# Pacing the early adding transfers by DVE's results as well as by ACT's copies

## The chip, the cores and the metric

The kernel runs on one core of one Trainium2 chip. Its engines run side by side, each with an instruction queue of its own: TensorE (PE, with its weight loads shown as PEld), VectorE (DVE), ScalarE (ACT), GpSimd (POOL) and SyncE (SP). SP issues most of the DMA transfers, POOL issues those that add into memory and some stores. The metric is the time of one execution on the device, in microseconds, as the median of several runs. Before the change it is 960.55 us (three runs, 957.44 to 962.81).

## The reference, cut to what matters

One encoder layer over 1024 tokens of width 1024, all in float32:

```python
h = rmsnorm(x, norm_g)
q, k, v, za, u, vs, zs, gm = split(h @ w_in)
a = window_sink_attention(rope(q), rope(k), v, sinks)       # 16 heads, 2 key heads, window 128
a = (a * silu(za)) @ w_att_out
s = chunked_spatial_gating(gelu(u), gelu(vs), sg_w, sg_b, ln_g, ln_b)
s = (s * silu(zs)) @ w_sg_out
ga, gs = split(sigmoid(gm + b_merge))
out = rmsnorm(x + (ga * a + gs * s) @ w_o, final_g)
```

## The kernel before, in words

Each float32 operand of a product is split into a high and a low part, so that one product of two matrices is three matmuls per slice. Large products are made in pairs of 128-row strips of the weights by a scheme with seven products in place of eight (`gemm_pair`). A product is 12 matmuls of 128x512 (L320), so a pair is 84. Seven forms of the activations (b11, t1, t2, b21, t3, b22, t4) are kept for a whole stage. Of the weights each pair needs seven forms too: four quarters that come from memory and four sums of them, one quarter being used in the sums alone.

The sums are made in one of two ways. `pair_job` loads the quarters into the buffers `wr` (there are three) and adds them on DVE (`sums`, L233 to L236), one pair or more ahead of use. The buffers and the splitting are driven by `split_next`, which is called at fixed places of a pair and, when few split strips are left, starts the next job: its loads are issued on SP as soon as a buffer is free, and its sums stand on DVE near the end of the pair. `early_job` does without DVE: its sums are made far ahead in device memory, by six DMA transfers on POOL, of which the later ones add to what lies there. Ten jobs are made this way, and the sums of the output weights (`o_sums`) by 16 further transfers: 76 in all, in the list `early`. The first read of a sum comes near the end of the attention stage, at 608.9 us.

The list is worked off at hooks, places behind each of the seven products of a pair (and in the first stage behind groups of products). `part_of_early` takes the next transfer from the list and issues it on POOL. So that the transfers do not all start at once, each waits for an instruction that was remembered last in `pace[0]` (`paced`, by a dependency with a semaphore). In `gemm_pair` the remembered ones are ACT's three copies out of PSUM: L338 after product 0, L342 after product 1, L345 after product 2. The results of products 3, 4 and 5 are added on DVE (L350, L355, L359), and product 6 goes to the stage's own `finish`.

The stages in order, with the times of the profiled execution: normalising, keys, values and the first half of the gate's input up to about 136 us (the early list starts at 92.6 us, one transfer at every second group of products, paced by PE); the U stage to about 229 us (four pairs, spatial mixing beside them, one transfer at every hook, through `both`); the Q stage without early transfers; then the attention stage, from about 330 to 645 us. There the attention of 16 heads is cut into steps (`attention`, a generator) that are worked in at the hooks of eleven pairs, and `part_of_early` is called at each hook from the second of these pairs on and issues a transfer at every second one. What follows (att-gate pairs, the two output projections and the last product with the residual) issues none.

Two more places read `pace[0]`. `gate_of` (L1222 and on) orders the sigmoid of a gate on ACT behind the last remembered instruction by an edge that gives order without a semaphore (`after`). And the last stage sets and reads it for itself.

On POOL, behind the early transfers, stand the stores of the attention's results (L1075), which wait for DVE's additions (L1073). On DVE, in the attention stage, stand the products' additions, the softmax's maximum (L1011) and scaling, the splits' low parts (L154) and the weight sums. The order of the instructions on each engine is made by the framework's planner from the written order, the dependencies and its estimates of durations; it need not be the written order.

Of the kernel before, what the change touches and what calls it, by code (L numbers as in the profile page):

```python
# [54 lines left out]
def hybrid_tile(  # L55
# [16 lines left out]
    nc = tc.nc  # L72
# [12 lines left out]
    def bank(tag, dt=F32):  # L85
        return psum.tile([P, 512], dt, name=nm("ps_" + tag), tag="ps_" + tag, bufs=2)

    def mtile(shape, dt, tag, bufs, pool=None):
        return (pool or main).tile(shape, dt, name=nm(tag), tag=tag, bufs=bufs)
# [7 lines left out]
    def xtile():  # L97
        return mtile([P, HALF], F32, "x", 5)
# [57 lines left out]
    def after(second, first):  # L156

        tc.add_manual_dep(
            second.ins,
            first.ins.name,  # L160
            mybir.DependencyInfo(mybir.DependencyClass.NoSync, mybir.DependencyReason.DATA),
            reason="order",
        )
# [41 lines left out]
    def split_next():  # L205

        if not units:
            begin_job()
        if not units:
            return  # L210
        halves, keys = units.pop(0)
        hi = mtile([P, D], F32R, "wh", 3)
        lo = mtile([P, D], F32R, "wl", 3)
        if isinstance(halves, list):
            for c, half in enumerate(halves):
                split(hi[:, half_of(c)], lo[:, half_of(c)], half)
        else:
            wide = halves.shape[1]
            split(hi[:, 0:wide], lo[:, 0:wide], halves)
        for c, key in enumerate(keys):  # L220
            ready[key] = hi[:, half_of(c)], lo[:, half_of(c)]
        if len(units) == 1:
            begin_job()
# [33 lines left out]

    early = []
    pace = [None]

    def paced(move):

        if pace[0] is not None:
            tc.add_manual_dep(
                move.ins,
                pace[0].ins.name,
                mybir.DependencyInfo(mybir.DependencyClass.Sync, mybir.DependencyReason.DATA),
                reason="pace",
            )
# [42 lines left out]
    def product(acc, part, form, fresh, last=True):  # L312
        wh, wl = part
        bh, bl = form
        for k in range(4):
            ks = slice(k * P, (k + 1) * P)
            for n, (lt, rt) in enumerate(
                ((wh[:, ks], bh[:, k, :]), (wh[:, ks], bl[:, k, :]), (wl[:, ks], bh[:, k, :]))
            ):
                nc.tensor.matmul(  # L320
                    acc,
                    lt,
                    rt,
                    start=fresh and k == 0 and n == 0,
                    stop=k == 3 and n == 2,
                    skip_group_check=True,
                )

    def gemm_pair(b, finish, hook=lambda: None, second="o"):

        n = done[0]
        done[0] += 1
        acc = bank("mm")[:]
        x11, x12, x22 = xtile(), xtile(), xtile()
        product(acc, ready[n, 0], b["b11"], True)
        pace[0] = nc.scalar.copy(x11[:], acc)  # L338
        hook()
        t5 = bank("o")[:]  # L340
        product(t5, ready[n, 2], b["t1"], True)
        pace[0] = nc.scalar.mul(x22[:], t5, -1.0)  # L342
        hook()
        product(acc, ready[n, 3], b["t2"], False)
        pace[0] = nc.scalar.copy(x12[:], acc)  # L345
        split_next()
        hook()
        t2 = bank(second)[:]
        product(t2, ready[n, 1], b["b21"], True)
        nc.vector.tensor_add(x11[:], x11[:], t2)  # L350
        finish(0, 0, x11, x11[:], 1.0)
        split_next()
        hook()
        product(acc, ready[n, 4], b["t3"], False)
        nc.vector.tensor_sub(x22[:], x22[:], acc)  # L355
        finish(1, 1, x22, x22[:], 1.0)
        hook()
        product(t5, ready[n, 5], b["b22"], False)
        nc.vector.tensor_add(x12[:], x12[:], t5)  # L359
        finish(0, 1, x12, x12[:], 1.0)  # L360
        split_next()
        hook()
        product(acc, ready[n, 6], b["t4"], False)
        finish(1, 0, xtile(), acc, -1.0)
        split_next()
        hook()
# [381 lines left out]
    def hook():  # L748
        for _ in range(2):
            if late:  # L750
                late.pop(0)()
# [69 lines left out]
    for m in range(0, KC, 2):  # L821

        def finish(i, half, q, src, sign, m=m):
            nc.scalar.activation(q[:], src, AF.Gelu, scale=sign)
            late.append(lambda: mix(m + i, half, q))

        if m % 4 == 0:
            late.append(lambda m=m: bias.append(bias_of(m // 4)))
        gemm_pair(hb, finish, both)
# [87 lines left out]
    for m in range(0, KC, 2):  # L917

        def finish(i, half, q, src, sign):
            if sign < 0:  # L920
                nc.scalar.mul(q[:], src, sign)
            put(q_raw, m + i, half, q[:])
            rows = slice((m + i) * P, (m + i + 1) * P)
            split_q(q[:], [(slice(0, P), q_hl[:, rows, half_of(half)].rearrange("a p t -> p a t"))])

        if m == 2:
            steps_of_q.append(rope_tables())
        if m == 4:
            steps_of_q.append(rotate(0))
        gemm_pair(hb, finish, part_of_q)  # L930
# [39 lines left out]
    def zs_pair(m, hook, *place):  # L970
        quarters = []
        gemm_pair(hb, lambda *quarter: quarters.append(quarter), hook)
        for i, half, q, src, sign in quarters:
            nc.scalar.activation(q[:], src, AF.Silu, scale=sign)
        for i, half, q, src, sign in quarters:
            g = get(s1_dr, m + i, half, *place)
            nc.vector.tensor_mul(q[:], q[:], g[:])
            put(s_dr, m + i, half, q[:])
# [243 lines left out]
    def gate_of(src, m, i, half, col):  # L1222

        g = gates.pop(0)
        c = col + m + i
        gate = nc.scalar.activation(g[:], g[:], AF.Sigmoid, bias=bm_sb[:, c : c + 1])

        after(gate, pace[0])
        return g

    def gated(q, src, sign, g):
# [6 lines left out]
    for m in range(0, KC, 2):  # L1238
        if m == 2:
            a_q = {}  # L1240
            ahead_of_time += loads_of_quarters(a_q, a_dr)
        if m == 6:
            a_forms = forms_of(a_q)
            next(a_forms)

        def finish(i, half, q, src, sign):
            gated(q, src, sign, gate_of(gs_dr, m, i, half, KC))
            put(y_dr, m + i, half, q[:], nc.gpsimd)
            gates.append(get(gs_dr, m + 2 + i, half, 4) if m < 6 else get(ga_dr, i, half, 4))

        gemm_pair(sb_, finish, part_of_loads, "tp")
# [58 lines left out]
    for m in range(0, KC, 2):  # L1310
        if m == 6:
            written[0] += 1
            had = [raw_tile() for _ in range(2)]
            for i in range(2):
                copy_to(had[i][:], y_dr[(m + i) * P : (m + i + 1) * P, :])

        def finish(i, half, q, src, sign):
            gated(q, src, sign, gate_of(ga_dr, m, i, half, 0))
            if m < 6:
                add_to(place(y_dr, m + i, half), q[:])  # L1320
                gates.append(get(ga_dr, m + 2 + i, half, 4))
            else:
                nc.vector.tensor_add(q[:], q[:], had[i][:, half_of(half)])
                if half == 1:
                    last_rows[i] = q
                copy_to(place(y_dr, m + i, half), q[:])

        if m == 2:
            ahead_of_time += [lambda name=name: load_o(name) for name in list(O_SOURCES)[:4]]
        gemm_pair(ab, finish, part_of_loads, "tp")  # L1330
# [22 lines left out]
    for p in range(4):  # L1353
        acc = bank("sc" if p < 2 else "mm")[:]
        x11 = mtile([P, HALF], F32, "g", 4, pool)
# [7 lines left out]
    for p in range(4):  # L1363
        n, t, acc, x11 = N_PAIRS + p, T_ORDER[p], accs[p], firsts[p]
# [6 lines left out]
        x12, x22 = xtile(), xtile()  # L1371
# [32 lines left out]
        t5 = bank("o")[:]  # L1404
# [129 lines left out]
```

## Time and profile before

| what | value |
|---|---|
| median of the runs | 960.55 us (957.44 to 962.81, three runs) |
| the profiled execution's own time | 963.5 us |
| its span, first to last instruction | 961.7 us |
| PE, DVE, ACT, POOL busy | 97%, 72%, 58%, 13% of the span |
| granted TensorE clock, mean | 0.993 |
| moved by DMA | 198.64 MB, mean 207 GB/s |
| of it by POOL's queue (q0), by SP's (q1) | 48.24 MB, 149.28 MB |
| early transfers | 40 + 20 into `sums`, 12 + 4 into `g` |

The page of a profile lists busy times by engine, the span in 40 slices, the DMA queues, the chain of work that ended last, and the costliest groups of instructions. Other views answer questions on a stretch: the table by stage (busy time of each engine, granted clock, DMA share and GB/s), who waited for whom, and the instructions in order of time. A row of the latter reads: start us, duration us, engine, line, operation, output<-input, shapes, count, and in brackets how long the engine stood idle before it and what ended that. PE's matmuls overlap, so a PE that is busy without a break is not for that reason at its peak, but an idle PE is time lost. A name such as `wr` is a tile by the program's name without its buffer number; `g` stands both for the gates' tiles and for the output weights' sums in memory.

### The profile page before, as it was taken

Reading aid. Unit: us, or ns where it says so; the run is one execution under the profiler, and the core shown is the slowest. Engines: PE = TensorE matmul, PEld = TensorE weight load, DVE = VectorE, ACT = ScalarE, POOL = GpSimd, SP = SyncE. Lnnn points to the kernel's source line nnn. Section 1 sums busy time; section 2 is a strip of 40 time slices with the busy share of each in tenths; the row PEclk is TensorE's granted clock in tenths of the full one; section 3 lists DMA queues with packets and bytes.
Section 4 is the critical chain, followed back from the end, with each engine's and each line's share of the span. In section 5 each row is a group of like instructions: output and inputs, shape, how many; then the busy total and the mean of one; then the engine's idle time right before and its main releaser. Section 6 shows DMA issues by size and latency. Waiting matters only on the chain.

```text
span 961.7 us, 13452 instructions
## 1 busy us (share of the span) xinstructions
PE 931.4 (97%) x4465; PEld 769.7 (80%) x4465; DVE 691.0 (72%) x1322; ACT 557.9 (58%) x1061; POOL 122.6 (13%) x202
## 2 busy tenths in 40 slices
PE   8999999999999999999999998999999999999996
PEld 6888888888878778788878886888887887787885
DVE  6655576666675778788878876755589489568985
ACT  7864343333444479977767675754475565457443
POOL 2111222220000001111101021000110011210011
PEclk9999999999999999999999998999999999999999
DMA  7444767887769557876566695849758757979732
GB/s 277 124 137 137 209 216 177 181 166 181 247 204 315 188 183 205 224 194 162 157 215 216 206 219 134 217 145 326 281 199 311 281 195 252 264 191 297 232 113 87
DMA packets 126550, 198.64 MB, mean 207 GB/s; under 512 B 11409, under 2 KB 59281, under 8 KB 126481
## 3 DMA queue, kind: packets, MB, share of 16 engines
q1 hardware_dynamic: 108864, 149.28, 46.8%
q0 software_dynamic: 17472, 48.24, 21.2%
q8 instruction: 35, 0.57, 0.3%
q14 instruction: 35, 0.28, 0.1%
q10 hardware_dynamic: 144, 0.26, 0.1%
HBM read 141.65 MB, written 85.46 MB: 236 GB/s over the span
## 4 chain that ended last, share of the span: by engine, by line
PE 44%; DVE 9%; DMA 5%; ACT 4%; issue 3%; SPq 0%; POOL 0%; DVEq 0%; POOLq 0%; ACTq 0%
PE ps_mm L320 18%; PE ps_o L320 15%; DMA wr<-in_w_dram 3%; PE ps_sc L1009 3%; PE ps_o L1068 2%; PE ps_tp L1049 2%; DVE wl L154 2%; PE ps_tp L320 2%; PE ps_sc L320 2%; DMA wr<-y_dr 1%; DVE bq L183 1%; ACT pr L1021 1%; ACT wh L153 1%; DVE T_b22l L154 0%; DMA g<-s_dr 0%
## 5 line engine op out<-in xcount | busy, mean ns | idle before, releaser
L153 ACT CAST wh<-s 128x1024 fp32r<-128x1024 f32 (+1 forms) x76 | 75.9, 1001 | 93.6 <-PE ps_mm L320 44.1
L153 ACT CAST wh<-wr 128x1024 fp32r<-128x1024 f32 (+1 forms) x78 | 64.4, 828 | 74.0 <-PE ps_mm L320 32.9
L154 DVE TENSOR_TENSOR wl<-wr,wh 128x1024 fp32r<-128x1024 f32 (+1 forms) x78 | 73.8, 948 | 44.4 <-ACT wh L153 43.8
L154 DVE TENSOR_TENSOR wl<-s,wh 128x1024 fp32r<-128x1024 f32 (+1 forms) x76 | 88.4, 1164 | 15.1 <-ACT wh L153 13.6
L1021 ACT ACTIVATE pr<-pr,sm 128x256 f32<-128x256 f32 (+1 forms) x128 | 62.5, 490 | 24.2 <-DVE sm L1011 23.8
L1011 DVE CUSTOM_DVE_ANT_0 pr<-ps_sc,mask,nsink_sb 128x256 f32<-128x256 f32 (+1 forms) x128 | 56.2, 462 | 14.2 <-PE ps_sc L1009 13.6
L320 PE MATMUL ps_o<-T_t1h,wh 128*128 128x512 f32 x144 | 57.3, 398 | 0.9 <-ACT wh L153 0.9
L320 PE MATMUL ps_mm<-T_t4h,wh 128*128 128x512 f32 x136 | 54.3, 399 | 3.8 <-DVE x L355 3.8
L320 PE MATMUL ps_mm<-T_b11h,wl 128*128 128x512 f32 x136 | 54.3, 399 | 3.3 <-DVE wl L154 3.3
L320 PE MATMUL ps_o<-T_b22h,wh 128*128 128x512 f32 x144 | 57.4, 399 | 0.0
L320 PE MATMUL ps_o<-T_b22h,wl 128*128 128x512 f32 x144 | 56.9, 395 | 0.0
L1009 PE MATMUL ps_sc<-k,q 128*128 128x256 f32 (+1 forms) x256 | 48.6, 295 | 8.3 <-DVE sm L1011 8.2
L1009 PEld LDWEIGHTS ps_sc<-k,q 128*128 128x128 f32 x256 | 40.6, 190 | 19.9 <-DVE sm L1011 15.9
L320 PE MATMUL ps_o<-T_b22l,wh 128*128 128x512 f32 x144 | 56.5, 393 | 0.0
L320 PE MATMUL ps_o<-T_t1h,wl 128*128 128x512 f32 x144 | 56.4, 391 | 0.1
L320 PE MATMUL ps_o<-T_t1l,wh 128*128 128x512 f32 x144 | 56.1, 390 | 0.0
L320 PE MATMUL ps_mm<-T_b11h,wh 128*128 128x512 f32 x136 | 54.7, 402 | 0.7 <-ACT wh L153 0.7
L320 PE MATMUL ps_mm<-T_b11l,wh 128*128 128x512 f32 x136 | 53.9, 396 | 0.0
L320 PE MATMUL ps_mm<-T_t2h,wh 128*128 128x512 f32 x136 | 53.4, 393 | 0.1
L320 PE MATMUL ps_mm<-T_t3h,wh 128*128 128x512 f32 x136 | 53.5, 394 | 0.0
L320 PE MATMUL ps_mm<-T_t4h,wl 128*128 128x512 f32 x136 | 53.2, 391 | 0.0
L320 PE MATMUL ps_mm<-T_t4l,wh 128*128 128x512 f32 x136 | 53.2, 391 | 0.0
(369 smaller groups left out, 2517.3 us busy)
## 6 DMA issues: line engine op xcount, KB each, us to landing
wr<-in_w_dram SPq DMA_DIRECT2D x82, 256.0 KB
sums<-in_w_dram POOLq DMA_DIRECT2D x20, 512.0 KB, 5.6
s<-sums SPq DMA_DIRECT2D x20, 512.0 KB
s_dr<-x SPq DMA_DIRECT2D x32, 256.0 KB
q_hl<-qhl SPq DMA_DIRECT2D x16, 512.0 KB
q<-q_hl SPq DMA_DIRECT2D x64, 128.0 KB
wr<-in_w_dram SPq DMA_DIRECT2D x14, 512.0 KB
y_dr<-x POOLq DMA_DIRECT2D x28, 256.0 KB, 5.6
```

Source lines behind the costliest of these rows:

```text
L153: nc.scalar.copy(hi, src)
L154: nc.vector.tensor_sub(lo, src, hi.bitcast(F32))
L183: op(dst[:, i : i + 2, :], a[:, i : i + 2, :], c[:, i : i + 2, :])
L320: nc.tensor.matmul(acc, lt, rt, start=fresh and k == 0 and n == 0, stop=k == 3 and n == 2, skip_group_check=True,)
L1009: nc.tensor.matmul(sc[:, js], qt[:, i, :], kt[:, f, k0:], start=f == 0, stop=f == 1)
L1011: nc.vector.tensor_tensor_reduce(pr[:, i, k0:], sc[:, js], mask[:, k0:], 1.0, nsink_sb[:, h : h + 1], op0=ALU.add, op1=ALU.min, accum_out= ...
L1021: nc.scalar.activation(pr[:, i, k0:], pr[:, i, k0:], AF.Exp, bias=nmax[:, i : i + 1], scale=-1.0, accum_out=sums[:, i : i + 1],)
L1049: nc.tensor.transpose(pt[:, i * P : (i + 1) * P], pr[:, i, kt * P : (kt + 1) * P], ident[:])
L1068: nc.tensor.matmul(po[:], vv, parts[kt][:, n, :], start=kt == tiles[0] and n == 0, stop=kt == 1 and n == 1)
```

## The change

The additions of products 3, 4 and 5 on DVE are remembered in `pace[0]` too, so that a transfer issued at a hook waits for the result of the product just in front of it. The last hook of a pair, behind product 6, has no result of its own to remember and waits for the addition of product 5. The gate's order on ACT is kept at the last copy (L345), through a new variable `copied`. The transfers, their order and their places in the list stay as they are.

```diff
     pace = [None]
+    copied = [None]
...
         product(acc, ready[n, 3], b["t2"], False)
-        pace[0] = nc.scalar.copy(x12[:], acc)
+        pace[0] = copied[0] = nc.scalar.copy(x12[:], acc)
         split_next()
         hook()
         t2 = bank(second)[:]
         product(t2, ready[n, 1], b["b21"], True)
-        nc.vector.tensor_add(x11[:], x11[:], t2)
+        pace[0] = nc.vector.tensor_add(x11[:], x11[:], t2)
         finish(0, 0, x11, x11[:], 1.0)
         split_next()
         hook()
         product(acc, ready[n, 4], b["t3"], False)
-        nc.vector.tensor_sub(x22[:], x22[:], acc)
+        pace[0] = nc.vector.tensor_sub(x22[:], x22[:], acc)
         finish(1, 1, x22, x22[:], 1.0)
         hook()
         product(t5, ready[n, 5], b["b22"], False)
-        nc.vector.tensor_add(x12[:], x12[:], t5)
+        pace[0] = nc.vector.tensor_add(x12[:], x12[:], t5)
         finish(0, 1, x12, x12[:], 1.0)
...
-        after(gate, pace[0])
+        after(gate, copied[0])
```

## The prediction

> **What bounds the kernel now.** I read the page first (busy shares), then the stages that hold the change, then who waited for whom in them, then the queues around the one stall that this shows.
>
> ```profile
> span 961.7 us, 13452 instructions
> ...
> PE 931.4 (97%) x4465; PEld 769.7 (80%) x4465; DVE 691.0 (72%) x1322; ACT 557.9 (58%) x1061; POOL 122.6 (13%) x202
> ```
>
> TensorE (PE) is busy for 931.4 of 961.7 us, so no change of pacing can win more than the 30 us in which it idles, plus what a lowered clock costs. The table by stage shows how little of that lies where the adding transfers run. Columns: stretch, length, then busy us of PE, PEld, DVE, ACT and POOL, granted clock, DMA share, GB/s.
>
> ```profile
> 136.00:217.00 81.00, 81.00 (x405) 67.88 (x405) 55.36 (x85) 28.20 (x41) 22.45 (x28) 1.00 0.79 174
> ...
> 340.00:360.00 20.00, 18.63 (x88) 15.20 (x88) 14.11 (x46) 16.76 (x43) 0.00 (x0) 0.91 0.59 193
> 360.00:412.00 52.00, 50.45 (x257) 41.81 (x256) 43.78 (x111) 50.98 (x104) 8.27 (x10) 1.00 0.79 212
> ...
> 570.00:580.00 10.00, 6.82 (x36) 5.43 (x34) 4.57 (x8) 4.60 (x8) 0.82 (x1) 0.95 1.02 306
> 580.00:590.00 10.00, 9.24 (x36) 7.65 (x37) 7.16 (x20) 4.78 (x15) 0.00 (x0) 0.71 0.08 24
> ```
>
> The U stage (136 to 217) has PE busy for all of its 81 us. The attention stage (about 340 to 645) loses 1.55 us of PE in 360 to 412 and 3.18 + 0.76 = 3.94 us in 570 to 590, where the granted clock also falls to 0.95 and 0.71: 0.5 + 2.9 = 3.4 us of full clock. That one place costs up to 7.3 us. Its chain:
>
> ```profile
> 568.76 0.68 DVE L355 TENSOR_TENSOR x<-x,ps_mm 128x512 f32<-128x512 f32 x1
> ...
> 572.27 0.69 DVE L359 TENSOR_TENSOR x<-x,ps_o 128x512 f32<-128x512 f32 x1 [1.17 <-PE ps_o L320]
> ...
> 574.27 1.28 DVE L154 TENSOR_TENSOR pT<-ps_tp,pT 128x512 fp32r<-128x512 f32 x2
> 579.61 0.69 DVE L233 TENSOR_TENSOR s<-wr 128x512 f32<-128x512 f32 x1 [4.06 <-DMA wr<-in_w_dram]
> ```
> ```profile
> 580.76 0.50 PEld L1009 LDWEIGHTS ps_sc<-k,q 128*128 128x128 f32 x2 [4.37 <-DVE sm L1011]
> ```
>
> DVE is done at 574.27 + 1.28 = 575.55, stands 4.06 us before the first sum of the next pair's weights (L233, waiting for a weight load), and the attention scores behind it on PE wait for DVE's maximum (L1011) queued after that sum. The load was issued at 570.86 and took 8.67 us; at 406.00 an equal one took 4.17:
>
> ```profile
> 570.86 8.67 DMA wr<-in_w_dram
> ```
> ```profile
> 406.00 4.17 DMA wr<-in_w_dram
> ```
>
> Why so long? POOL's queue, how long its three transfers took, and the two DMA queues from 570 to 572 (packets, MB, share of the time of 16 engines):
>
> ```profile
> 562.16 2.52 POOL L412 DMA_DIRECT2D g<-in_w_dram  x3 [7.55 <-ACT x L345]
> 571.40 0.82 POOL L1075 DMA_DIRECT2D at_dr<-aT  x1 [6.72 <-DVE aT L1073]
> ```
> ```profile
> DMA to landing us min/median/max: 7.2/9.2/12.1
> ```
> ```profile
> q0 software_dynamic: 99, 0.34, 99.7%
> q1 hardware_dynamic: 36, 0.02, 5.0%
> ```
>
> ACT's copy at L345 released three 512 KB adding transfers at once. Issued at 562.16, 562.72 and 563.25 they landed after 7.2, 9.2 and 12.1 us, that is at 569.3, 571.9 and 575.3, some 2.5 to 3.4 us each. While they ran, POOL's queue (q0) had the DMA engines and the loads of SP's queue (q1) moved at 5%.
>
> **The change, part by part.** In each pair of products the places ("hooks") after products 0, 1, 2 stay paced by ACT's L338, L342, L345. Those after products 3, 4, 5 now wait for DVE's L350, L355, L359, and the one after product 6 for L359; before, these four all counted from L345.
>
> *Which transfers move.* In the U stage each hook issues one: four pairs by four late hooks are 16. In attention every second hook issues one: nine pairs with two late ones each are 18. Of 76 early transfers 34 move; the list's order stays.
>
> *The waits themselves.* Up to 34 more semaphore waits on POOL, at 17 ns (first row below) 0.6 us on an engine that is 13% busy: nothing. Behind a waiting transfer on POOL stand only the 16 stores of attention results.
>
> ```profile
> L277 POOLq EVENT_SEMAPHORE  x30: 17/17/17, 111.6 to 474.6; - x30
> ```
> ```profile
>   DVE aT L1073: 76.6, 11
> ```
>
> The second row says that these stores themselves wait for DVE (76.6 us in 11 waits), for an addition that stands behind the pacing one on the same engine, so the new wait is over first: nothing, at most one issue of 0.82 us, covered by the second aT buffer. If that cover went, the next write of aT would be late by that much.
>
> *U stage.* Five transfers, all issued from L345 on within 4.16 us (first row below), would go one or two at a time over about 10 us.
>
> ```profile
> 166.01 4.16 POOL L277 DMA_DIRECT2D sums<-in_w_dram  x5 [2.24 <-ACT x L345]
> ```
> ```profile
> DVE s L233 <- DMA wr<-in_w_dram: 7.8, 3, 4.9
> ```
>
> DVE's wait for weights there (7.8 us in three waits) may shrink, but PE is busy 81.00 of 81.00: no gain. A loss needs DVE to fall behind by more than the 25.6 us that it idles there (81.00 - 55.36); I take 0.
>
> *The stall at 570.* The second and third transfer wait for L355 and L359: issued near 569.4 and 573.0 instead of 562.7 and 563.3. The first alone is over by about 568, so the loads held in SP's queue can move before the second starts. SP issues the last load no earlier, since it follows in order:
>
> ```profile
> 570.42 0.38 SPq L427 DMA_DIRECT2D ga_dr<-x  x1
> 570.86 0.67 SPq L197 DMA_DIRECT2D wr<-in_w_dram  x1
> ```
>
> It now meets the second transfer and the attention store of 571.40. Bounds: as quick as the load of 406.00, 4.17 us, landing at 575.0, before DVE wants it: the whole 7.3 us won. As slow as now, if second, store and third all go ahead: 0 won. I take 6 us, nearer the quick end because one transfer of about 3 us stands in front where three stood: landing at 576.9, 1.3 us of DVE wait left, as much PE idle, and a short fall of the clock. In 340 to 360, where PE also idled 1.37 us, the clock of 0.91 cost 1.8 us; the stretch is another, so I count half, 0.9. Left: 1.3 + 0.9 = 2.2; won: 7.3 - 2.2, about 5 us.
>
> A rule bears on this. The Trainium skill, "DMA: Bandwidth & Descriptors", section "Queues, rings and completion order", says that a DMA engine takes turns between the queues it has work for, a packet at a time. By that the load would have had about half of the engines however many transfers POOL had queued, spreading them would change nothing, and the sum would be 0. The 5.0% against 99.7% above is not half, so here I go by the rows.
>
> *The pair from 389 to 412.* Here the late transfer moves towards the load that waits least comfortably:
>
> ```profile
> 399.20 0.68 DVE L355 TENSOR_TENSOR x<-x,ps_mm 128x512 f32<-128x512 f32 x1
> ...
> 401.21 0.69 DVE L350 TENSOR_TENSOR x<-x,ps_o 128x512 f32<-128x512 f32 x1 [1.33 <-PE ps_o L320]
> ...
> 404.43 0.68 DVE L359 TENSOR_TENSOR x<-x,ps_o 128x512 f32<-128x512 f32 x1
> ...
> 410.29 0.69 DVE L233 TENSOR_TENSOR s<-wr 128x512 f32<-128x512 f32 x1 [0.35 <-DMA wr<-in_w_dram]
> ```
> ```profile
> 395.58 2.47 POOL L277 DMA_DIRECT2D sums<-sums  x3 [4.59 <-ACT x L345]
> ```
>
> Three 256 KB transfers start at 395.58; the third would now be issued at 404.43 + 0.68 = 405.1, just ahead of the load of 406.00 that DVE already waits 0.35 us for. By size it takes about half of 2.5 to 3.4 us. The load comes at most 1.7 us later, or not later at all, since SP's queue is relieved of the same work from 397 to 403. With the clock's share of 0.9 the loss is 0 to 2.6; I take 1.
>
> *The other seven attention pairs.* Of DVE's waits for weight loads in 340 to 650 only two stand, 4.4 us together, and both are accounted for above:
>
> ```profile
> DVE s L233 <- DMA wr<-in_w_dram: 4.4, 2, 4.1
> ```
>
> In those pairs the third transfer arrives after L359, about when the last loads land. I take 0; one such collision would cost 1.5 to 3.4 us of DVE plus 0.9 to 3.4 of clock.
>
> *The sigmoid gate.* It followed the last copy at L345 and, through the new `copied`, still does: 0.
>
> *Order.* L355 runs before L350 at 399.20 although it is written after it: the framework plans each engine's order from its estimates, and 34 new edges enter that plan. No row prices this; bounds are the best and the worst place of the stage, -7.3 and +7.3; I take 0.
>
> Sum: 0 - 5 + 1 = -4 us. The profiled execution took 963.5 us (span 961.7), so 959.5 for one like it; that is 2.95 above the median 960.55, and the lowest run (957.44) leaves room for the stall to be shorter in some. On the median: 956.6, say 957.
>
> **The rivals.**
>
> *Nothing won* (960.5). The second transfer, the store of 571.40 and the third hold the load to 579 all the same. For it: q1's 5.0%; the third transfer would start just as the store ends. Against: at 406.00 a load with SP's queue full but POOL's idle took 4.17.
>
> *Slower, about 967.* The transfer behind L359 comes one product before the weight sums and collides with the last loads of several pairs. Decides: a weight load issued after L359 minus 2 us, or landing less than 3 us before L233, in two or more pairs. Price: two collisions of 3.4 + 1.5 are 9.8 us, less 3 of the 5 won: 960.55 + 6.8. For it: the 0.35 us at 410.29. Against: in the pair at 551 the loads are issued before L359.
>
> *All won, about 953.* 7.3 us, no new wait: 953.3. It needs the load in 4.7 us or less.
>
> **How the numbers follow.** Chances: forecast 0.45, nothing won 0.20, slower 0.27, all won 0.08. What a measurement here tells from no change is about 0.5%, 4.8 us: 955.75 and 965.35 are the bounds. Of the forecast's own range, 953.5 to 960, somewhat under half lies below 955.75: faster 0.22 + 0.08 = 0.30; slower 0.26; the rest, 0.44, within. The range from 951 to 967 takes in the bounds of the stall and up to the slower case's middle.
>
> **What would show it.** POOL's rows: no group of x3 behind L345, single transfers with L350, L355, L359 as releasers. At 570: an L233 wait below 2 us, a load under 6.5 us, the clock above 0.9 in both stretches. At 410: the wait at L233 under 2 us. The U stage still full. I am wrong if PE's idle time in attention grows at L233 or L1011 in pairs that have none now, or if the order on DVE and PE differs widely.

## The result, and the profile after

The changed kernel takes 967.24 us (median of six runs, 965.88 to 972.25) against 959.69 us for the kernel before (six runs, 957.44 to 962.81). The ratio is 1.0069, with a 95% interval of 1.0046 to 1.0092: slower by 0.7%, or 4.4 to 8.9 us on 963, where 957 was forecast. The two profiled executions stand closer together than the medians, 963.5 before and 965.9 after: the former was the slowest run of its kernel and the latter the fastest of its own. The later comparisons ran on other chips, on which the kernel before took 963.1 to 964.9 us; each ratio below is against its own chip.

The page of the profile after, busy shares:

```profile
span 964.1 us, 13477 instructions
...
PE 931.0 (97%) x4465; PEld 768.3 (80%) x4465; DVE 691.7 (72%) x1322; ACT 557.9 (58%) x1061; POOL 121.8 (13%) x202
```

No engine does more work, so what was lost is PE's idle time, and time at a lowered clock. The table by stage after (stretch, length, busy us of PE, PEld, DVE, ACT, POOL, granted clock, DMA share, GB/s):

```profile
136.00:217.00 81.00, 81.00 (x405) 67.86 (x405) 55.48 (x85) 27.97 (x40) 19.23 (x25) 1.00 0.83 175
340.00:360.00 20.00, 18.45 (x95) 14.76 (x96) 14.98 (x48) 17.81 (x46) 0.00 (x0) 1.00 0.54 168
...
380.00:430.00 50.00, 45.16 (x228) 36.78 (x227) 38.49 (x97) 42.11 (x95) 6.99 (x9) 1.00 0.70 181
550.00:600.00 50.00, 45.22 (x226) 37.16 (x225) 35.31 (x97) 32.40 (x84) 5.82 (x8) 0.93 0.66 163
570.00:580.00 10.00, 8.47 (x43) 6.75 (x42) 5.79 (x12) 5.27 (x9) 2.48 (x3) 1.00 0.93 250
580.00:590.00 10.00, 6.75 (x27) 5.69 (x28) 5.84 (x13) 2.77 (x9) 0.00 (x0) 0.66 0.40 113
```

The same two wide stretches before:

```profile
380.00:430.00 50.00, 48.29 (x247) 40.07 (x246) 42.26 (x108) 45.38 (x98) 8.24 (x10) 1.00 0.79 197
550.00:600.00 50.00, 46.06 (x227) 37.76 (x227) 35.41 (x100) 32.07 (x85) 8.30 (x10) 0.93 0.69 170
```

The U stage is as full as it was. From 380 to 430 PE idles 4.84 us instead of 1.71. The stall near 580 has not gone: 4.78 us of PE instead of 3.94, with the same clock of 0.93. From 340 to 360 the clock is 1.00, where it was 0.91 before; other runs of either pacing have that drop or not. By such differences ahead of 380 the profile after is 3.0 us in front when it comes to the pair at 389, which is why the two profiled executions differ by less than the medians.

On PE, DVE, ACT and SP the instructions stand in the same order in both kernels; on POOL only five places differ, where a store of attention results has changed places with one or two early transfers. So what differs is when the transfers start. POOL's queue after, around the two places (start, duration, line, what, count, idle time before and its releaser):

```profile
392.50 0.83 POOL L278 DMA_DIRECT2D sums<-sums  x1 [4.58 <-ACT x L346]
397.09 0.81 POOL L278 DMA_DIRECT2D sums<-sums  x1 [3.76 <-DVE x L356]
402.39 0.80 POOL L278 DMA_DIRECT2D sums<-sums  x1 [4.49 <-DVE sm L1036]
...
412.60 0.84 POOL L278 DMA_DIRECT2D sums<-sums  x1 [6.59 <-ACT x L343]
...
563.80 0.87 POOL L413 DMA_DIRECT2D g<-in_w_dram  x1 [7.54 <-ACT x L346]
571.39 0.82 POOL L413 DMA_DIRECT2D g<-in_w_dram  x1 [6.72 <-DVE sm L1036]
573.08 0.82 POOL L1076 DMA_DIRECT2D at_dr<-aT  x1 [0.87 <-DVE aT L1074]
574.91 0.84 POOL L413 DMA_DIRECT2D g<-in_w_dram  x1 [1.01 <-DVE x L360]
```

No group of three is left: each transfer goes where the change puts it. Twice the view names L1036, a neighbour on DVE, as the releaser; but 402.39 is 0.30 us behind the end of the addition at L360 (401.41 + 0.68), and 571.39 is 0.30 us behind that at L356 (570.41 + 0.68), as 574.91 is behind L360. What the weights then did shows in the chain of the profile after, at both places:

```profile
402.99 6.37 DMA wr<-in_w_dram
...
414.90 5.55 DMA g<-s_dr
...
572.51 4.09 DMA wr<-in_w_dram
576.60 0.61 DVE pT L154
577.21 4.89 issue
582.10 0.18 DVE s L233
```

and on DVE:

```profile
401.41 0.68 DVE L360 TENSOR_TENSOR x<-x,ps_o 128x512 f32<-128x512 f32 x1
...
409.49 0.69 DVE L233 TENSOR_TENSOR s<-wr 128x512 f32<-128x512 f32 x1 [2.57 <-DMA wr<-in_w_dram]
...
420.48 0.69 DVE L978 TENSOR_TENSOR x<-x,g 128x512 f32<-128x512 f32 x1 [3.28 <-DMA g<-s_dr]
...
582.10 0.69 DVE L233 TENSOR_TENSOR s<-wr 128x512 f32<-128x512 f32 x1 [4.90 <-issue]
```

In the pair that stood at 389 to 412, the third transfer starts at 402.39, 0.6 us ahead of the weight load of 402.99. That load takes 6.37 us (4.17 before) and DVE waits 2.57 us for it (0.35). Everything behind it on DVE is late, so the stores of this pair's results and, behind them on SP, the load of `g` (here a part of the spatial mixing's result, by which DVE multiplies) start late too: at 414.90, 2.3 us behind the next pair's transfer of 412.60. It takes 5.55 us, and DVE waits another 3.28. Before, transfer and load started together:

```profile
415.61 0.84 POOL L277 DMA_DIRECT2D sums<-sums  x1 [6.59 <-ACT x L342]
```
```profile
415.71 3.98 DMA g<-s_dr
```
```profile
419.72 0.69 DVE L977 TENSOR_TENSOR x<-x,g 128x512 f32<-128x512 f32 x1 [1.72 <-DMA g<-s_dr]
```

Near 580 the chain ends the load at 576.6 and calls the rest "issue", time for which it knows no releaser. The load was not over then: going by the times at which its semaphore was raised, its 16 parts came from 579.4 to 582.0, the last 9.5 us after the issue, where it was 8.67 before.

### The profile page after: what moved, and what is told of

It is laid out like the page before. It is cut to its first block, busy times and chain, and to the rows that moved or that the text cites. A ratio compares the mean times of both kernels' runs of the same rounds, so it can differ in the third digit from the quotient of the medians.

```text
span 964.1 us, 13477 instructions
## 1 busy us (share of the span) xinstructions
PE 931.0 (97%) x4465; PEld 768.3 (80%) x4465; DVE 691.7 (72%) x1322; ACT 557.9 (58%) x1061; POOL 121.8 (13%) x202
## 4 chain that ended last, share of the span: by engine, by line
PE 41%; DVE 10%; DMA 6%; issue 3%; ACT 3%; SPq 0%; DVEq 0%; ACTq 0%
PE ps_mm L321 17%; PE ps_o L321 14%; PE ps_sc L1010 3%; DVE wl L154 2%; PE ps_o L1069 2%; PE ps_tp L1050 2%; DMA wr<-in_w_dram 2%; PE ps_sc L321 2%; PE ps_tp L321 2%; DMA g<-s_dr 1%; DMA g<-ga_dr 1%; DVE bq L183 1%; DMA wr<-y_dr 1%; ACT wh L153 1%; DMA q<-q_hl 1%
## 5 line engine op out<-in xcount | busy, mean ns | idle before, releaser
L321 PE MATMUL ps_mm<-T_t3h,wl 128*128 128x512 f32 x136 | 53.1, 391 | 0.0
```

Of the source, the lines that this page charges most:

```text
L321: nc.tensor.matmul(acc, lt, rt, start=fresh and k == 0 and n == 0, stop=k == 3 and n == 2, skip_group_check=True,)
```

## The experiments

*How they are read.* Single executions scatter: the kernel before alone ranged from 958.5 to 968.4 us on one of the chips. So beside the ratios there is a second measure. Since the order on DVE is the same everywhere, the start of one DVE addition in a trace, minus the start of the same one in the trace of before, is the delay there; its rise from 402 to 440 us is what the pair at 389 and the one after it lost, and its rise from 567 to 592 what the stall lost, against the profile of before. All traces stand in a table behind the experiments.

All kernels below but the first have this helper; the set `by_dve[0]` says after which products the DVE result paces, and the empty set is the pacing before:

```diff
+    by_dve = [(3, 4, 5)]
+    def added(place, ins):
+        if place in by_dve[0]:
+            pace[0] = ins
...
-        pace[0] = nc.vector.tensor_add(x11[:], x11[:], t2)
+        added(3, nc.vector.tensor_add(x11[:], x11[:], t2))
```

**The kernel before once more.** No edit.

> The kernel before, profiled once more. If its profiled execution of 963.5 us was an ordinary one, a second one shows the same two costs: DVE's wait of 4.06 us at the weight sum near 580 us and a fallen clock there. If it was an unlucky one, the span is nearer 958 us, and the wait near 580 is shorter than 2 us or the clock stays up in 340 to 360.

One run, 967.9 us, 4.4 above the profiled one. By the delay it lost -0.1 and 1.5 us at the two places and 2.5 us between 800 and 950, where no early transfer runs. So a single trace tells a few microseconds from nothing only where it is read place by place.

**Which stage.** The change in the U stage alone, then in the attention stage alone:

```diff
     (u_only)
+    by_dve[0] = ()
     parts = attention()
     (att_only)
-    by_dve = [(3, 4, 5)]
+    by_dve = [()]
...
+    by_dve[0] = (3, 4, 5)
     parts = attention()
```

> Only the 16 transfers of the U stage are paced by DVE's results; in the attention stage all late hooks count from L345 as before. Theory (late transfers run into the last weight loads of the attention stage): PE is busy throughout the U stage, so the time is that of the kernel before, 960 us, ratio 0.997 to 1.003. Rival (the U stage's transfers, pushed into the Q stage, cost the time): 964 to 967. Rival (the 34 waits themselves cost something, each the same): 16 of 34 of 7.5 us, 963.5.

> Only the 18 transfers of the attention stage are paced by DVE's results. Theory: the whole change, 966 to 968 us, with DVE's wait for a weight load near 410 us above 2 us. Rival (U stage): 960. Rival (each wait costs the same): 18 of 34, 964.

U stage alone: 962.64 us, ratio 0.9981 (0.9960 to 1.0003). Attention alone: 969.91 us, 1.0051 (1.0028 to 1.0075). The loss is made in the attention stage, and the U stage carries none that can be told from nothing.

**One pair.** The change in the pair from 389 to 412 alone:

```diff
-        zs_pair(m, lambda: part_of_attention(m), 2)
+        by_dve[0] = (3, 4, 5) if m == 6 else ()
+        zs_pair(m, lambda: part_of_attention(m), 2)
+    by_dve[0] = ()
```

> DVE's results pace only the two late transfers of one attention pair, the one that runs from about 389 to 412 us. Theory (its third transfer, issued just ahead of the last weight load, delays that load and the load of g behind it): PE's idle time in 380 to 430 rises from 1.7 us to 4.5 to 5 as in the changed kernel, 550 to 600 stays as before (3 to 5 us idle, clock 0.93), and the time is about 3 us above the kernel before. Rival (the loss is spread over many pairs): 380 to 430 stays under 2.5 us and the time within 1 us of before.

967.05 us, 1.0043 (1.0015 to 1.0070). One pair of nine, with two late transfers, gives most of the loss. PE idles 4.80 us from 380 to 430, as in the full change.

**Which of the late transfers.** DVE's pacing in attention after product 5 only, and after 3 and 4 only:

```diff
     (last_only)
+    by_dve[0] = (5,)
     parts = attention()
     (mid_only)
+    by_dve[0] = (3, 4)
     parts = attention()
```

> In the attention stage only the last transfer of a pair is moved (behind L359); the one behind products 3 or 4 still counts from L345. Theory: it is the last one that collides, so 380 to 430 shows 4 to 5 us of PE idle time. Near 580 the load meets one transfer and the attention store instead of two and the store: a wait of 2 to 4 us. Rival (the middle one collides): 380 to 430 under 2.5 us.

> In the attention stage the late transfers of a pair count from L350 or L355 at the latest, none from L359. Theory: the pair at 389 to 412 issues its last two transfers about 5 us ahead of the last weight load, 380 to 430 shows under 3 us of PE idle time; near 580 two transfers start together just ahead of the load, so the stall there is at least as long as before. Rival (the middle one collides): 380 to 430 shows 4 to 5 us.

One run each: 967.21 and 972.92 us. Both lose at the first place (5.4 and 6.8 us by the delay), so there any of these late transfers is enough; that the last one alone collides, as was expected, is not so. They part at the second: with two transfers together and the third behind product 5 there is no stall (DVE waits 0.55 us, where 2 to 4 were expected) and the clock stays at 1.00 in 550 to 600; with one first and two later, PE idles 7.11 us there.

**Not later but earlier.** The pacing as before, but the transfers issued at the hooks after products 0, 1 and 2, in all pairs, or in the eight pairs from the fourth on, or so without the one that meets the `g` load:

```diff
     (at_front; mix and mix2 do so in the eight gs and ga pairs only,
      mix2 at the places 2 and 3 in the first of them)
     def part_of_attention(m=KC):
-        if m > 2:
-            part_of_early()
+        place, pair = at[0] % 7, at[0] // 7
+        at[0] += 1
+        if m > 2 and (place < 3 or place == 3 and pair > 8):
+            part_of_early(1)
```

> Pacing as before (ACT's copies), but in the attention stage the transfers are issued behind products 0, 1 and 2 of each pair, one each (two pairs issue one more behind product 3), so that none stands behind L350, L355 or L359 and no three start together at L345. Theory: the loads issued after product 2 meet at most one transfer, the waits near 410 and 580 are under 1 us, 954 to 958 us. Rival (any transfer in this stage costs about the same wherever it is put, since the DMA engines are the limit): 959 to 962. Rival (they now run into the loads of queries and keys): above 962.

> Pacing by ACT's copies. The first two attention pairs with early transfers (the zs pairs) issue at the places of the kernel before, the eight pairs after them behind products 0, 1 and 2, one each. Theory: 380 to 430 costs what it did before (1.7 us of PE idle time, clock 1.00), 550 to 600 is free of the stall as with the front places, and the time is 0.6 to 1.0% below the kernel before. Rival (the cost moves to another pair whatever is done): within 0.5% of before.

> Pacing by ACT's copies. The zs pairs as in the kernel before; in the pair after them no transfer ahead of product 2, then two; the seven pairs after that one each behind products 0, 1 and 2. Theory: 380 to 430 under 2 us of PE idle time with the clock at 1.00, 550 to 600 under 1 us, 0.7 to 1.2% below the kernel before, about 953 to 956 on a chip where that takes 962. Rival (something else of the list collides in turn): not more than 0.6% below.

961.48 us, 0.9950 (0.9916 to 0.9984); 958.13 us, 0.9941 (0.9912 to 0.9970); 957.43 us, 0.9934 (0.9911 to 0.9957). The stall at 580 is gone in all three (PE idles at most 0.41 us, clock 1.00). The first two lose 5.3 and 5.8 us at the first place, where DVE waits 5.4 and 4.4 us for `g`: two transfers now start ahead of that load, by 0.2 to 0.5 and by 2.4 to 2.8 us. That had not been expected, and at_front missed its 954 to 958 us by it. In the third, where none does, the wait is 1.4 and PE idles 1.39 us.

**The change without its two places.** The pair at 389 paced as before, and in the pair from 551 to 586 only the last transfer by DVE:

```diff
+        by_dve[0] = () if m == 6 else (3, 4, 5)
         zs_pair(m, lambda: part_of_attention(m), 2)
...
+            by_dve[0] = (5,) if dst is ga_dr and m == 2 else (3, 4, 5)
             gemm_pair(hb, rest(dst, m), part_of_attention)
```

> The changed kernel, but with ACT's pacing for the pair at 389 to 412, and in the pair at 551 to 586 only the last transfer behind DVE. Theory (the whole loss comes from the first of these pairs, and the second keeps its old stall only because its middle transfer is moved too): 380 to 430 shows about 1.7 us of PE idle time, 550 to 600 under 1 us with the clock at 1.00, and the time is 0.5 to 0.8% below the kernel before. Rival (other late transfers cost as well): within 0.3% of before.

956.65 us, 0.9922 (0.9894 to 0.9950): faster than both kernels. So the changed pacing of all other pairs and of the U stage costs nothing that can be told here.

**The transfer of 412.60 taken out of the way.** The change, but with its first transfer in the pair behind moved from behind product 1 to behind product 2:

```diff
+        if pair >= 0 and place in ((2, 3, 5) if pair == 2 else (0, 2, 4, 6) if pair % 2 else (1, 3, 5)):
+            part_of_early(1)
```

> The changed kernel, but in the pair after the one at 389 to 412 the first transfer waits for product 2 instead of product 1. Theory (the late weight load shifts the load of g into this transfer, and that makes some 1.5 us of the 3.1 lost): DVE's wait for g falls from 3.3 us to under 2, PE's idle time in 380 to 430 from 4.8 to about 3.3 us. Rival (the wait for g has its length from the transfer before): no change.

One run, 972.03 us. At the place itself it went as the second step of the reading above asks. DVE's waits from 395 to 430 in this kernel:

```profile
DVE s L233 <- DMA wr<-in_w_dram: 2.6, 1, 2.6
...
DVE x L982 <- DMA g<-s_dr: 1.3, 1, 1.3
```

The weight load is as late as in the change (2.6 us of wait), but `g` now takes 1.3 us of wait in place of 3.3, and PE idles 3.02 us in place of 4.84. By the delay the place still costs 3.8 us in place of 4.4, since in this trace the clock was at 0.66 from 415 to 420, where it is 1.00 after. What it lost elsewhere it lost at the stall (7.64 us of wait with the same order of transfers) and after 700 us, where no early transfer runs: 4.9 us by the delay, of which I know no cause.

**The two places, one by one.** How the loss divides between them was open after these runs. Three more: the change in the pair from 551 to 586 alone; the kernel before with that pair's third transfer alone behind product 5; and the change without the pair at 389.

```diff
     (ga2_only, on the pacing before)
+            by_dve[0] = (3, 4, 5) if dst is ga_dr and m == 2 else ()
             gemm_pair(hb, rest(dst, m), part_of_attention)
     (ga2_split, on the pacing before)
+            by_dve[0] = (5,) if dst is ga_dr and m == 2 else ()
             gemm_pair(hb, rest(dst, m), part_of_attention)
     (but_m6, on the change)
+        by_dve[0] = () if m == 6 else (3, 4, 5)
         zs_pair(m, lambda: part_of_attention(m), 2)
```

> The change in one pair alone, the one from 551 to 586; all others as before. If the change does nothing there (the first theory: stall neither removed nor worse), the time is that of the kernel before, within 1.5 us, and the wait of DVE's first weight sum near 580 lies between 3.2 and 5.2 us, as in the four looks with ACT's pacing. If it makes the stall worse (second theory: waits of 4.9, 5.7, 6.1 and 7.6 us in four looks with the change's pacing of it, 2 us more on average), the wait is about 6 and the time 2 to 3 us above before.

> The kernel before, but in the pair from 551 to 586 the last of the three transfers alone waits for product 5's addition; no other pair is touched. If the stall is the whole difference between the fastest version and the kernel before, the first weight sum near 580 does not wait, the clock stays at 1.00 in 550 to 600, and the time is 6 to 7.5 us below before. If the pacing of the other pairs by DVE's results wins something of its own, it is less than that, by that much.

> The change, but in the pair from 389 to 412 the pacing as before. If that pair is the whole loss, the time is that of the kernel before, within 1.5 us, with 1.5 to 2 us of PE idle in 380 to 430 (the change: 4.84). If the change also makes the stall near 580 worse, 2 to 3 us above before remain.

970.14 us, 1.0056 (1.0018 to 1.0093); 956.84 us, 0.9930 (0.9906 to 0.9954); 966.07 us, 1.0017 (0.9993 to 1.0041). The change makes the stall worse, not only no better. That is read from the traces; the last ratio alone, with 1 in its interval, does not show it. From 550 to 600 in the kernel with the change there alone, then without the pair at 389, then with the split:

```profile
550.00:600.00 50.00, 42.93 (x211) 35.34 (x210) 34.83 (x92) 30.16 (x78) 5.81 (x7) 0.93 0.58 144
```
```profile
550.00:600.00 50.00, 42.99 (x213) 35.30 (x212) 32.70 (x92) 31.10 (x83) 6.62 (x8) 0.93 0.69 170
```
```profile
550.00:600.00 50.00, 49.38 (x254) 40.71 (x253) 39.61 (x112) 36.16 (x95) 8.25 (x10) 1.00 0.81 194
```

PE idles 7.07, 7.01 and 0.62 us. The split kernel's POOL queue and DVE show why:

```profile
561.54 1.70 POOL L417 DMA_DIRECT2D g<-in_w_dram  x2 [7.57 <-ACT x L350]
570.76 0.82 POOL L1080 DMA_DIRECT2D at_dr<-aT  x1 [7.52 <-DVE aT L1078]
572.62 0.84 POOL L417 DMA_DIRECT2D g<-in_w_dram  x1 [1.04 <-DVE x L364]
```
```profile
575.65 0.69 DVE L233 TENSOR_TENSOR s<-wr 128x512 f32<-128x512 f32 x1 [0.75 <-DVE pT L154]
```

Two transfers start early enough to be all but done (they land at 567.9 and 571.8), the third comes 1.9 us behind the last weight load (issued at 570.73). The view names DVE itself for the 0.75 us ahead of the first sum, but by its semaphore the load's last part came at 575.57, 0.08 us before that sum, the same distance as before and after. So the load took 4.84 us in place of 8.67, and DVE waited 0.75 us in place of 4.06. One transfer later and the stall is back: the change put the second at 571.39, 1.1 us ahead of that load. Removing the stall is worth 6.7 us (0.7% of 963; 4.4 to 9.1 by the interval), and the 7.5 us of the fastest kernel differ from it by less than either is known.

The kernel with the change near 580 alone came out above its expectation, and its profile says where: it lost 4.6 us at the first place too, where it paces as before. There, by chance, POOL's transfer led the `g` load by 0.49 us:

```profile
415.02 0.84 POOL L278 DMA_DIRECT2D sums<-sums  x1 [6.59 <-ACT x L347]
```
```profile
415.51 6.56 DMA g<-s_dr
```

In the kernel without the pair at 389 the lead was 0.36 us and the load took 4.11:

```profile
412.07 0.84 POOL L278 DMA_DIRECT2D sums<-sums  x1 [6.59 <-ACT x L347]
```
```profile
412.43 4.11 DMA g<-s_dr
```

**All traces at the two places.** Delay in us against the profile of before, as explained at the start; "ACT" is the pacing before, "DVE" the change's, and a lead is by how much POOL's last transfer started ahead of the `g` load:

| kernel | pair at 389 | lead; DVE's wait for `g` | 402 to 440 | pair at 551 | 567 to 592 |
|---|---|---|---|---|---|
| before | ACT | 0.10; 1.7 | 0 | ACT | 0 |
| before_again | ACT | -0.12; 1.7 | -0.1 | ACT | +1.5 |
| u_only | ACT | 0.28; 1.8 | +0.7 | ACT | -0.6 |
| ga2_split | ACT | -0.06; 1.8 | 0.0 | split | -5.7 |
| all_but_two | ACT | -0.35; 1.4 | -0.5 | split | -5.7 |
| but_m6 | ACT | 0.36; 1.8 | +0.9 | DVE | +2.5 |
| ga2_only | ACT | 0.49; 4.3 | +4.6 | DVE | +2.9 |
| after | DVE | 2.30; 3.3 | +4.4 | DVE | +0.4 |
| att_only | DVE | 2.37; 2.9 | +4.8 | DVE | +1.9 |
| m6_only | DVE | 1.75; 3.5 | +5.0 | ACT | -1.0 |
| gs_held | DVE | none; 1.3 | +3.8 | DVE | +3.4 |
| last_only | last | 2.32; 3.3 | +5.4 | split | -5.9 |
| mid_only | middle | 1.31; 4.4 | +6.8 | one, two | +2.1 |
| at_front | front | 0.18 (and 2.44); 5.4 | +5.3 | front | -6.3 |
| mix | ACT | 0.53 (and 2.76); 4.4 | +5.8 | front | -5.9 |
| mix2 | ACT | none; 1.4 | -0.5 | front | -6.4 |

Three times the change's own pacing at the first place cost 4.4 to 5.0 us; in the seven traces with the pacing before there and the next pair's transfer behind product 1, it was -0.5 to 0.9 six times and once 4.6. At the second place the change (with mid_only, which leaves one first and two later) gives +0.4 to +3.4 in six traces, 2.2 on average; the pacing before -1.0 to +1.5 in four, 0.0 on average. So the change costs about 4 to 5 us at the first place and 2 at the second, 6 to 7 together; measured were 6.6 (0.69% of 963; 4.4 to 8.9).

The delays at the second place can be added up from the traces. The granted clock stood at 0.50 from 579.0 to 585.9 before, and from 580.6 to 587.5 after. PE's idle time, plus half of such a spell where PE is busy, makes 3.94 + 2.55 = 6.5 us before, 4.78 + 2.10 = 6.9 after, 9.0 without the pair at 389, and 0.6 with the split. Against before, these sums give the delays of the last column within 0.2 us in all traces.

## Why the prediction was wrong, point by point

*The U stage, 0: right within what was measured.* PE is busy 81.00 of 81.00, and the stage alone gave a ratio of 0.9981 with 1 just inside its interval. A gain of some 2 us behind it stays open: from 240 to 290 PE idles 1.0 to 1.2 us in all five traces with the change there, 2.12 in that of before and 0.7 to 3.3 in the other ten. At 389 the five are 2.9 to 3.5 us ahead of the trace of before; but of the ten, at_front, mix and mix2 are 2.2 to 3.3 ahead too.

*The waits themselves, 0: right.* POOL waits by 17 ns semaphores as before and is 13% busy; the pairs other than the two named lost nothing that can be told (the fastest kernel keeps the change in them).

*The order, 0, with bounds of 7.3 either way: right.* It is the same on every engine but POOL.

*The other seven pairs, 0: right*, by the same kernel.

*The stall at 570, 5 won: wrong, and so was its lower bound of 0.* The starts were right: second and third transfer were put at 569.4 and 573.0 and came at 571.39 and 574.91, in a trace that runs 1.65 us late there. What failed is the step "nearer the quick end because one transfer of about 3 us stands in front where three stood". The load that counts is issued 1.1 us after the second transfer, and that one, the store and the third all stand beside it. Nor is a transfer over in about 3 us: that was the spacing at which three queued ones landed. With the loads beside it the second took 7.49 us from issue to landing, until 578.9, and the last load 9.5 where 6 were taken. "As slow as now" was no bound: with three together at 562 the first two are done by 572, with one first and two later they are not, and DVE waited 4.9, 5.7, 6.1, 7.1, 7.2 and 7.6 us where it waits 3.2 to 5.2 with the pacing before. The rival "nothing won" named the cause; the size was 2 us worse. The 7.3 us as the worth of the whole stall were somewhat much: it is 6.5 by the sum above, since 0.9 of the clock's 3.4 us fell while PE stood idle anyway, and 5.7 to 6.4 by the delays where the stall is gone.

Here the rule that I weighed against the trace came nearer with its number, 0, than the row I chose. By the Trainium skill, "DMA: Bandwidth & Descriptors", section "Queues, rings and completion order", a DMA engine takes turns between the queues that it has work for, a packet at a time. From 573 to 579 after, the shares of the two queues (packets, MB, share of 16 engines' time) do lie near each other:

```profile
q0 software_dynamic: 214, 0.77, 59.6%
q1 hardware_dynamic: 686, 0.82, 43.3%
```

But the packets that the profile counts, 214 to 686, do not alternate one by one (whether they are what the rule calls packets is not shown here). Nor did half of the engines for the load follow from turns: from 570 to 572 before, by the rows in the prediction, one packet of POOL's queue took 322 ns of an engine and one of SP's 44. And the 5.0% that I went by was a stretch of two microseconds and no measure of what the load would get: from 572 to 580 SP's queue had 76.6%. What I had drawn from the rule, that spreading changes nothing, is not so in general: the split, with nothing of POOL's waiting ahead of the load, won 6.7 us.

*The pair from 389 to 412, 1 lost, bounds 0 and 2.6: wrong in size.* The mechanism was the one described: the transfer lands just ahead of the load, which comes 2.2 us later in place of "at most 1.7". Left out was what the lateness does next. The `g` load behind it moves into the next pair's transfer, which it had so far started level with, and DVE waits 1.6 us more for it. At the following weight load, near 437, come 0.6 us of wait, where there was none. The pair costs 4 to 5 us. The bound counted one load; the edit moves all that SP issues behind it.

*The rivals.* "Slower, about 967" came out to the microsecond, but that is luck: its mechanism had collisions in several pairs and kept part of the 5 won. It was one pair with two waits, and a stall made worse.

*What would show it.* The single transfers with their DVE releasers and the full U stage came. The wait at L233 near 570 was to be below 2 us, the load under 6.5, the clock above 0.9 in both stretches: 4.90, 9.5 and 0.66. The wait at 410 was to be under 2: 2.57. It was to be wrong "if PE's idle time in attention grows at L233 or L1011 in pairs that have none now"; it grew at L233 in the two pairs that were named, and at the `g` addition, which I had not listed.

## What to carry to other kernels

A transfer spread out over a stage must be placed against the loads that are waited for, one by one: start it when it will be over by the time the last of them is issued, or behind it, not just ahead (here 0.5 to 2.4 us ahead was too close). An edit that makes one load late moves every load behind it in the same queue; follow these into what they meet next, since the second collision cost 1.6 us here where the first cost 2.2. And "no better than now" is a bound only if the new order puts no more beside the load than the old.

## What the runs showed of the hardware that was not expected

The wait for the `g` load jumps with POOL's lead. In all traces in which the one transfer near it started less than 0.4 us ahead of the load, or behind it, DVE waited 1.4 to 1.8 us for `g`; at leads of 0.49 and 1.31 it waited 4.3 and 4.4, and at 1.75 to 2.37 from 3.5 down to 2.9. By the chain of the profile the load took 3.98 and 4.11 us at leads of 0.10 and 0.36, and 6.56 at 0.49. With leads of 0.10 and -0.12 in its two traces the kernel before stands 0.3 to 0.6 us from that edge; how much of its scatter this makes is not shown. That the edge itself is the cause was not tried by moving the load alone, only by taking the transfer away (1.3 us of wait).

Each kernel whose PE idles 3 us or more near 580 runs at a clock of 0.90 to 0.97 in 550 to 600, and each in which the stall is gone at 1.00. The fall comes in whole spells: in the ten traces with a stall the clock was at 0.50 for 3.4 us (once), 6.8 (eight times, as from 580.6 to 587.5 after) or 10.2 (once), starting 2.0 to 4.8 us after PE fell idle. So a gap here costs its own length, and half of the part of the spell that lies behind it. Elsewhere it is less regular: from 380 to 430 PE idles 4.8 us after with the clock at 1.00.
